# Key-query products of two heads issued alternately on 32-column tiles, decayed operands in two products, and one rounded gate product

## The chip, the cores and the metric

The kernel runs on one core of a Trainium2 chip. The engines of that core are TensorE (PE in the profile; PEld is its loading of weights), VectorE (DVE), ScalarE (ACT), GpSimd (POOL) and SyncE (SP), which issues DMAs. They run side by side and meet through semaphores. The metric is the device time of one execution in microseconds; the figure for a kernel is the median of its runs.

## The reference, cut to what matters

One layer of a streaming encoder is computed for 1024 prompt tokens and 32 sample tokens. The change lies in its gated linear attention: four heads, key width 64, value width 128, with a decay for each token and key channel.

```python
glog = jax.nn.log_sigmoid((glr @ w_gate2 + b_gate2)) / GLA_GATE_TEMP      # glr: 16 columns of h @ w_in
b = jnp.cumsum(g, axis=2)
o_inter = jnp.einsum('bhid,bhde->bhie', q * jnp.exp(b), S)
diff = b[:, :, :, None, :] - b[:, :, None, :, :]
decay = jnp.exp(jnp.where(causal[None, None, :, :, None], diff, -jnp.inf))
att = jnp.einsum('bhid,bhjd,bhijd->bhij', q, k, decay)
o = o_inter + jnp.einsum('bhij,bhje->bhie', att, v)
S_new = jnp.exp(b_last[:, :, 0, :])[..., None] * S + jnp.einsum('bhjd,bhje->bhde', k * jnp.exp(b_last - b), v)
```

Around it stand the input projection (queries, keys, values, an output gate, a second group of mixers), the output projection and an MLP of width 4096 with two LayerNorms.

## The kernel before

The kernel has three stages. The first (up to about 115 us in the profile) normalizes the input and forms part of the projections. The second, in which the change lies, forms the rest of the projections, runs the attention and begins the output projection; it ends near 407 us. The third does the remaining output projection and the MLP, up to 1218 us. Big products keep each operand as a rounded high part and a rest (type fp32r) and take three passes; small ones are plain fp32, and the profile records two matmuls (and two weight loads) for each plain fp32 product, one for an fp32r product.

Tokens are cut into three blocks of 384, 384 and 288, and a block into windows: eight windows of 128 prompt tokens and one of 32 sample tokens. The four heads are two pairs (pair 0, pair 1), so there are 18 rounds of window and pair. Windows are numbered 0 to 8 here; in pair 0 they run first. Two heads of a pair lie on partitions 0 to 63 and 64 to 127.

- `gate` makes, for a block and pair, the running sum of log decays (`b`) and differences inside groups of four (`dd`): a product of 16 by 128 weights with 384 columns (L703), three ACT functions, and a row of DVE work.
- `elem` makes the decayed queries and keys of a window. For each of five levels (blocks of 64, 32, 16, 8, 4 tokens) POOL subtracts running sums (L748, L749), one ACT exponential covers all levels (L755, shown under the helper's line L608; 128x640), and DVE multiplies the later half of each block by the queries (L761) and the earlier half by the keys (L762). `x` holds four more products. `z` and `x` share the buffer `zx`, of which there are two, so `elem` of window n+2 starts when window n is done with its buffer.
- `gram` makes the attention matrix: for each head, 16 products of 32x32 at levels 16, 8, 4 and inside the groups of four (L783), one of 64x64 (L786) and two of 32x32 (L790), all on 64 rows of the PE array. The PE then transposes the decayed keys (L793). DVE picks the causal parts out of PSUM under masks into `cmp` (L797), copies the four diagonal blocks into `att` (L805), ACT copies one off-diagonal block (L800) and DVE two (L802).
- `outp` makes the state increment (L817), the part of the output from the state (L821) and from `att` (L824), and updates the state on DVE (L830). `gla_norm` normalizes (ACT, POOL), the PE transposes (L851), and DVE multiplies into `mix` (L854).
- `mix_split` splits `mix` into high and rest (ACT L943, DVE and POOL L944) for the output projection.
- `ada_stream` (114 to 203 us) streams 24 weight tiles through the buffers `wad` and `zx` and reduces them on DVE.

The order on the PE is written out by a planner (`Order`): each part of the work is a stream with a priority, and a `yield (a, b)` says that it took the PE a nanoseconds and wants to go on b nanoseconds later; in between, streams of lower priority (projections) put their matmuls. These matmuls are called fill here. The order on DVE, ACT and POOL comes from the framework's scheduler, which uses its own estimate of times. Each engine runs its instructions strictly in its order.

## Time and profile before

| | |
|---|---|
| median of 3 runs | 1217.69 us (1216.70 to 1219.08) |
| the profiled execution's own time | 1219.88 us |
| its span in the profile | 1218.1 us |
| mean granted PE clock | 0.98 |
| PE busy | 1169.3 us, 96% of the span |
| DVE busy | 909.8 us, 75% |
| first and last key-query product | 240.7 and 384.8 us |

The page gives busy time by engine, the span in 40 slices, the DMA queues, a chain of waits and the costliest groups of instructions. A busy PE is one with some matmul in flight; matmuls overlap, so the length of a piece of PE work is read from one start to the next. In rows of instructions in order of time the columns are start and length in us, engine, line, operation, output<-inputs, array rows*columns, shapes, count, and in brackets the idle time before and what ended it.

### The profile page before, as it was taken

The numbers are of one execution on the slowest core, as the hardware profiler recorded it, in microseconds if no ns is written. First come the engines' busy times: TensorE is split into PE (matmuls) and PEld (weight loads), VectorE is DVE, ScalarE is ACT, GpSimd is POOL, SyncE is SP. The second block draws the span as 40 slices with busy tenths as digits, with TensorE's granted clock in tenths as the row PEclk, the third lists the DMA queues.
The fourth block names the chain that finished last, engine by engine and source line by source line (L and its number), as shares of the span: only waits on it lengthen the run. The fifth ranks groups of instructions, "written<-read, shape, count | busy, mean of one in ns | idle before, by whom it ended". The sixth has DMA issues, their size and how long they took to land.

```text
span 1218.1 us, 22199 instructions
## 1 busy us (share of the span) xinstructions
PE 1169.3 (96%) x8539; PEld 1114.4 (91%) x8539; DVE 909.8 (75%) x1905; ACT 521.2 (43%) x1065; POOL 469.4 (39%) x682
## 2 busy tenths in 40 slices
PE   5999999999899999899989999999999999999996
PEld 3678999988788999799989999999999999999996
DVE  5664797579896688756759769589499597697577
ACT  4462322446566665642425343343443443433321
POOL 2443110345684154348541442334414414422034
PEclk9999999999899999889989999999999999999998
DMA  9632564110012765204762672743825726737412
GB/s 370 239 126 90 180 214 125 36 36 20 23 37 76 263 219 165 83 31 169 251 242 70 210 252 91 244 171 120 300 100 184 265 70 207 246 100 226 157 73 104
DMA packets 49498, 188.46 MB, mean 155 GB/s; under 512 B 5328, under 2 KB 10928, under 8 KB 49392
## 3 DMA queue, kind: packets, MB, share of 16 engines
q1 hardware_dynamic: 31824, 97.38, 23.4%
q0 software_dynamic: 17568, 89.66, 21.5%
q8 instruction: 67, 1.10, 0.4%
q14 instruction: 39, 0.32, 0.1%
HBM read 171.36 MB, written 15.66 MB: 154 GB/s over the span
## 4 chain that ended last, share of the span: by engine, by line
PE 76%; DVE 11%; DMA 4%; POOL 3%; ACT 2%; issue 2%; SPq 0%; POOLq 0%; DVEq 0%; ACTq 0%
PE mm L250 26%; PE mm L1375 16%; PE mm L1442 12%; PE mm L1236 9%; PE mm L284 3%; PE zp L284 3%; DVE hl L1039 2%; DMA raw<-in_w_dram 2%; DVE acc L1467 1%; DMA wst<-in_w_dram 1%; PE zp L250 1%; DMA tdT<-hl 1%; PE mm L1142 1%; PE gt L783 1%; PE mm L227 1%
## 5 line engine op out<-in xcount | busy, mean ns | idle before, releaser
L1038 ACT CAST hl<-raw 128x512 fp32r<-128x512 f32 (+1 forms) x238 | 143.7, 613 | 242.9 <-PE mm L1442 93.3
L1039 DVE TENSOR_TENSOR hl<-raw,hl 128x512 fp32r<-128x512 f32 (+1 forms) x238 | 203.5, 861 | 40.8 <-ACT hl L1038 40.8
L1375 PE MATMUL mm<-ring,hl 128*128 128x384 f32 x960 | 173.7, 338 | 3.4 <-DMA ring<-tdT 3.4
L1375 PEld LDWEIGHTS mm<-ring,hl 128*128 128x128 f32 x960 | 168.9, 190 | 3.8 <-issue 3.7
L1442 PE MATMUL mm<-ring,hl 128*128 128x384 f32 x792 | 140.8, 335 | 1.3 <-DVE acc L1467 1.3
L1442 PEld LDWEIGHTS mm<-ring,hl 128*128 128x128 f32 x792 | 137.5, 188 | 1.9 <-ACT ring L1038 1.4
L250 PE MATMUL mm<-hT,whl 128*128 128x384 f32 (+1 forms) x792 | 129.0, 322 | 0.0
L250 PEld LDWEIGHTS mm<-hT,whl 128*128 128x128 f32 x792 | 127.0, 188 | 1.1 <-issue 1.1
L250 PE MATMUL mm<-h,hl 128*128 128x288 f32 (+1 forms) x756 | 122.3, 318 | 1.7 <-POOL h L239 1.4
L250 PEld LDWEIGHTS mm<-h,hl 128*128 128x128 f32 x756 | 115.4, 196 | 4.6 <-POOL h L239 3.6
L1083 POOL TENSOR_TENSOR raw<-raw 128x512 f32<-128x512 f32 x26 | 35.9, 1383 | 184.7 <-DMA raw<-in_w_dram 155.3
L1467 DVE SCALAR_TENSOR_TENSOR acc<-mm,G,acc 128x384 f32<-128x384 f32 x162 | 93.7, 607 | 5.4 <-PE mm L1442 4.8
L1236 PE MATMUL mm<-fb,hl 128*128 128x288 f32 x708 | 97.0, 295 | 0.0
L1236 PEld LDWEIGHTS mm<-fb,hl 128*128 128x128 f32 x708 | 95.4, 188 | 0.0
L1247 DVE SCALAR_TENSOR_TENSOR acc<-mm,G,acc 128x256 f32<-128x256 f32 (+3 forms) x176 | 61.8, 390 | 12.0 <-PE mm L1236 11.8
L250 PE MATMUL mm<-mhl,hl 128*128 128x384 f32 (+1 forms) x384 | 65.3, 325 | 2.0 <-ACT hl L1038 1.8
L250 PEld LDWEIGHTS mm<-mhl,hl 128*128 128x128 f32 x384 | 60.3, 192 | 2.6 <-ACT hl L1038 2.1
L1323 POOL DMA_DIRECT2D ring<-tdT x56 | 31.3, 560 | 71.8 <-PE mm L1375 38.2
L284 PE MATMUL zp<-zvw,hT 128*128 128x512 f32 x192 | 52.9, 418 | 4.5 <-ACT hT L236 4.5
L1399 DVE TENSOR_TENSOR tmps<-mm,tmps 128x384 f32<-128x384 f32 x28 | 15.6, 558 | 50.4 <-PE mm L1375 50.4
L1345 ACT CAST ring<-F 128x768 fp32r<-128x768 f32 x42 | 35.1, 837 | 40.0 <-DVE F L1337 20.0
L217 POOL TENSOR_SCALAR rs<-mv 128x1 f32<-128x1 f32 (+1 forms) x27 | 8.6, 322 | 111.1 <-DVE mv L216 108.5
(253 smaller groups left out, 2282.2 us busy)
## 6 DMA issues: line engine op xcount, KB each, us to landing
ring<-tdT POOLq DMA_DIRECT2D x56, 768.0 KB, 5.9
raw<-in_w_dram SPq DMA_DIRECT2D x80, 512.0 KB, 3.9
ring<-tdB POOLq DMA_DIRECT2D x42, 768.0 KB, 6.4
wst<-in_w_dram SPq DMA_DIRECT2D x34, 512.0 KB, 4.4
wad<-in_w_dram POOLq DMA_DIRECT2D x24, 512.0 KB, 4.6
tdT<-hl SPq DMA_DIRECT2D x16, 384.0 KB, 2.9
st<-in_w_dram SPq DMA_DIRECT2D x10, 512.0 KB, 10.2
tdB<-h SPq DMA_DIRECT2D x6, 768.0 KB, 4.4
```

The lines of the kernel that those rows point to most:

```text
L250: PE.matmul(pt[:, :n], h[:, a, 128 * kk:128 * kk + 128], act[:, b_, k, :n], start=(i == 0 and j == 0), stop=(i == 7 and j == 2))
L284: PE.matmul(pt[:n, :width], act[:, a, k, off:off + n], hl[:, b_, width * kk:width * kk + width], start=(k == 0 and a + b_ == 0), stop=(k = ...
L1038: S.copy(hl[:, 0, :n], src)
L1039: V.tensor_tensor(hl[:, 1, :n], src, hl[:, 0, :n].bitcast(F32), ALU.subtract)
L1083: G.tensor_tensor(s, a21, a22, ALU.add)
L1236: PE.matmul(pt[:, :n], hl[kk // 2][:, a, o_:o_ + 128], f(kk)[:, c_], start=(kk == 0 and j == 0), stop=(kk == 3 and j == 2))
L1247: V.scalar_tensor_tensor(ac, pt[:, o + lo - p0:o + hi - p0], G2[:, m, c:c + 1], ac, ALU.mult, ALU.add)
L1323: G.dma_start(s, td[t, j].rearrange("p (a c) -> p a c", a=2))))
L1345: S.copy(q[:, 0], src)
L1375: PE.matmul(pt[:, :384], hl[:, a, o_:o_ + 128], quad(ts[j])[:, b_, kk], start=first and j + kk + i == 0, stop=j + kk + i == 4, skip_group_ ...
L1442: PE.matmul(pt[:, :384], hl[:, a, o_:o_ + 128], f[:, b_, kk], start=first and kk + i == 0, stop=kk + i == 3, skip_group_check=True)
L1467: V.scalar_tensor_tensor(ac, v, G2[:, m, 0:1], ac, ALU.mult, ALU.add)
```

## The change

Four things change, all in the second stage.

1. In `gram` the products of the two heads alternate, product by product, and all of them use tiles of 32 columns: the 64x64 product becomes two of 32x64. The diagonal blocks are put into `att` by one product of `cmp` with a block-diagonal matrix of ones (`bd`), which writes all of `att`; the copies of the off-diagonal blocks follow it.
2. In `elem` the ten half-block multiplications become two over all levels: queries times `z` into a new buffer `zq` (there is one), keys times `z` in place. Both halves are now computed, and the products read the half they need.
3. In `gate` the low-rank activations are kept as a rounded high part (twice) and a rest, stacked on 96 partitions against high, high and rest of the weights, so that one fp32r product of 96 rows takes the place of one plain fp32 product of 16 rows. For pair 0 this adds an ACT copy and a DVE subtraction per block.
4. The planner is told that a key-query round takes 950 (700 for the window of 32) in place of 1700, and that `outp` comes 3800 in place of 3200 later. To make room, `b` has 3 buffers in place of 4 and `wad` 1 in place of 2, with more of the weight tiles going through `zx`.

```diff
-            wg2 = pb.tile([96, 256], F32, name="wg2")
+            wg2 = pb.tile([P, 2, 128], F32, tag="on", name="wg2", bufs=2)[:96].rearrange("p a b -> p (a b)")
...
-            glr = pb.tile([96, 384], F32, name="glr")
+            bd = pb.tile([P, 1, 4, 32], F32, name="bd")
+            glr = [pb.tile([96, BLK[b][1]], F32R, name=f"glr{b}") for b in range(3)]
+            wsp = pb.tile([96, 256], F32R, name="wsp")
...
+                S.copy(wsp, wg2)
+                V.tensor_tensor(wsp[64:96], wg2[64:96], wsp[64:96].bitcast(F32), ALU.subtract)
...
-                        V.tensor_copy(glr[r, :n], pt[:16, :n])
-                        yield 330, 1000
+                        gl = glr[b]
+                        V.tensor_copy(gl[0:16], pt[:16, :n])
+                        S.copy(gl[64:80], pt[:16, :n])
+                        V.tensor_tensor(gl[32:48], pt[:16, :n], gl[0:16].bitcast(F32), ALU.subtract)
+                        yield 330, 1500
                     pt = mm()
-                    PE.matmul(pt[:, :n], wg2[r, 128 * p:128 * p + 128], glr[r, :n], start=True, stop=True,
-                              tile_position=(32 * b, 0))
+                    PE.matmul(pt[:, :n], wsp[:, 128 * p:128 * p + 128], glr[b], start=True, stop=True)
...
-                    bb = pb.tile([P, 384], F32, tag="b", name="b", bufs=4)
+                    bb = pb.tile([P, 384], F32, tag="b", name="b", bufs=3)
...
-                for i in range(l0, 5):
-                    s = LV[i]
-                    zz = zs[i - l0]
-                    V.tensor_tensor(zz[:, :, 1], zz[:, :, 1], hv(q, s)[:, :, 1], ALU.mult)
-                    V.tensor_tensor(zz[:, :, 0], zz[:, :, 0], hv(k, s)[:, :, 0], ALU.mult)
+
+                zq = pb.tile([P, 5, 128], F32, tag="zq", name="zq", bufs=1)
+                lv = lambda t: t.rearrange("p (o t) -> p o t", o=1).to_broadcast([P, 5 - l0, w])
+                V.tensor_tensor(zq[:, l0:5, :w], z[:, l0:5, :w], lv(q), ALU.mult)
+                V.tensor_tensor(z[:, l0:5, :w], z[:, l0:5, :w], lv(k), ALU.mult)
...
-                for hd in range(2):
-                    r = slice(64 * hd, 64 * hd + 64)
-                    for li in range(4):
-                        kz, qz = (z[:, li + 2], z[:, li + 2]) if li < 3 else (x[:, 1], x[:, 0])
-                        for g in range(w // 32):
-                            cs = slice(32 * g, 32 * g + 32)
-                            PE.matmul(gt[32 * g:32 * g + 32, hd, 32 * li:32 * li + 32], kz[r, cs], qz[r, cs],
-                                      start=True, stop=True, tile_position=(64 * hd, 32 * g))
-                    if w == 128:
-                        PE.matmul(gt[0:64, hd, 128:192], z[r, 0, 0:64], z[r, 0, 64:128],
-                                  start=True, stop=True, tile_position=(64 * hd, 0))
...
+                def grams(kz, qz, parts):
+
+                    for o_, cs, d_ in parts:
+                        for hd in range(2):
+                            r = slice(64 * hd, 64 * hd + 64)
+                            PE.matmul(gt[o_:o_ + 32, hd, d_:d_ + cs.stop - cs.start], kz[r, o_:o_ + 32], qz[r, cs],
+                                      start=True, stop=True, tile_position=(64 * hd, o_))
+                for li in range(4):
+                    grams(*((z[:, li + 2], zq[:, li + 2]) if li < 3 else (x[:, 1], x[:, 0])),
+                          [(o_, slice(o_, o_ + 32), 32 * li) for o_ in range(0, w, 32)])
+                if w == 128:
+                    grams(z[:, 0], zq[:, 0], [(o_, slice(64, 128), 128) for o_ in (0, 32)])
+                    grams(z[:, 1], zq[:, 1], [(o_, slice(o_ + 32, o_ + 64), 192) for o_ in (64, 0)])
...
+                    V.tensor_tensor(att.rearrange("p h (c t) -> p h c t", c=4), cmp.rearrange("p h (c t) -> p h c t", c=1)
+                                    .to_broadcast([P, 2, 4, 32]), bd.to_broadcast([P, 2, 4, 32]), ALU.mult)
...
-                for g in range(w // 32):
-                    V.tensor_copy(att[32 * g:32 * g + 32, :, 32 * g:32 * g + 32], cmp[32 * g:32 * g + 32])
+                else:
+                    V.tensor_copy(att[:32, :, :32], cmp[:32])
...
-                        yield (1700 if w == 128 else 1700), 200
+                        yield (950 if w == 128 else 700), 200
...
-                        yield 0, 3200
+                        yield 0, 3800
...
-                    if i % 4 < 2:
-                        w = pb.tile([P, D], F32, tag="wad", name="wad", bufs=2)
+                    if i % 3 == 0:
+                        w = pb.tile([P, D], F32, tag="wad", name="wad", bufs=1)
```

The order of instructions moves in three places. The first is one round of key-query products on the PE (a window of 128); `gt` is the PSUM tile they write, and L793 (now L800) is the transpose behind them. Before:

```order
L783 MATMUL gt<-zx 32x32 x16
L786 MATMUL gt<-zx 64x64
L790 MATMUL gt<-zx 32x32 x2
L783 MATMUL gt<-zx 32x32 x16
L786 MATMUL gt<-zx 64x64
L790 MATMUL gt<-zx 32x32 x2
L793 MATMUL mm<-ident,zx 128x128
```

Now:

```order
L791 MATMUL gt<-zq,zx 32x32 x24
L791 MATMUL gt<-zx 32x32 x8
L791 MATMUL gt<-zq,zx 32x64 x4
L791 MATMUL gt<-zq,zx 32x32 x4
L800 MATMUL mm<-ident,zx 128x128
```

The 38 products have become 40, and no product uses 64 columns of the array.

The second is the PE around the `outp` of window 4 of pair 1, where `hs` and `mhl` are operands of fill (values of the last window, and the output projection). Before, 16 matmuls with `hs` (their last row stands here) and 12 with `mhl` lie between the key-query round and `outp`:

```order
L276 MATMUL mm<-whl,hs 64x256
L250 MATMUL mm<-mhl_3832,whl 128x384 x12
L817 MATMUL mm<-v,ks 64x128 x2
L821 MATMUL o<-st_1223,zx 128x256
L824 MATMUL o<-v,att_1211 128x128 x2
L783 MATMUL gt<-zx 32x32 x16
L786 MATMUL gt<-zx 64x64
L790 MATMUL gt<-zx 32x32 x2
L783 MATMUL gt<-zx 32x32 x16
L786 MATMUL gt<-zx 64x64
L790 MATMUL gt<-zx 32x32 x2
L793 MATMUL mm<-ident,zx 128x128
```

Now (the first three rows are `outp` of window 3, then the round of window 4 and its `outp`):

```order
L826 MATMUL mm<-v,ks 64x128 x2
L830 MATMUL o<-st_1227,zx 128x256
L833 MATMUL o<-v,att_1214 128x128 x2
L791 MATMUL gt<-zq,zx 32x32 x24
L791 MATMUL gt<-zx 32x32 x8
L791 MATMUL gt<-zq,zx 32x64 x4
L791 MATMUL gt<-zq,zx 32x32 x4
L800 MATMUL mm<-ident,zx 128x128
L860 MATMUL o<-ident,on 128x128 x2
L826 MATMUL mm<-v,ks 64x128 x2
L830 MATMUL o<-st_1227,zx 128x256
L833 MATMUL o<-v,att_1215 128x128 x2
```

Window 4 has no fill now; window 3 has 12 matmuls of it, and the windows before took more than they did.

The third is DVE at the same window 4 of pair 1. Before, from the products of window 5 to the copies of two off-diagonal blocks of window 4 (L802):

```order
L761 TENSOR_TENSOR zx<-zx,q 128x64
L762 TENSOR_TENSOR zx<-zx,k 128x64
L761 TENSOR_TENSOR zx<-zx,q 128x2x32
L762 TENSOR_TENSOR zx<-zx,k 128x2x32
L761 TENSOR_TENSOR zx<-zx,q 128x4x16
L762 TENSOR_TENSOR zx<-zx,k 128x4x16
L761 TENSOR_TENSOR zx<-zx,q 128x8x8
L762 TENSOR_TENSOR zx<-zx,k 128x8x8
L761 TENSOR_TENSOR zx<-zx,q 128x16x4
L762 TENSOR_TENSOR zx<-zx,k 128x16x4
L141 TENSOR_TENSOR whl<-wst,whl 128x512 x2
L802 COPY att_1211<-gt 32x2x32 x2
```

Now, from the masked picks of window 4 to the same copies (L811), with `zq` (L769) and the key product (L770) of window 5, the first products of window 6 (L764, L765) and the state update of window 4 (L839) ahead of them:

```order
L804 COPY_PREDICATED cmp_1217<-msk,gt 128x64 x2
L769 TENSOR_TENSOR zq<-zx,q 128x640
L807 TENSOR_TENSOR att_1215<-cmp_1217,bd 128x256
L839 SCALAR_TENSOR_TENSOR st_1227<-st_1227,el,mm 64x128 x2
L953 TENSOR_TENSOR mhl_3669<-mix_859,mhl_3669 128x384
L770 TENSOR_TENSOR zx<-zx,k 128x640
L764 TENSOR_TENSOR zx<-zx,q 128x128
L765 TENSOR_TENSOR zx<-zx,k 128x128
L811 COPY att_1215<-gt 32x2x32 x2
```

Ten products have become two, and the copies that `outp` waits for stand behind more work of later windows than before.

More of the change, by code (lines that the diff above doesn't have):

```diff
@@ L599, in consts_b @@
                 G.memset(cb_[:, 0:1], 1.0)
-                for t in att_t + cmp_t:
+                for t in att_t + cmp_t + [g_.bitcast(F32) for g_ in glr] + [bd]:
                     G.memset(t, 0.0)
+                for g in range(4):
+                    G.memset(bd[32 * g:32 * g + 32, :, g], 1.0)
+                S.copy(wsp, wg2)
+                V.tensor_tensor(wsp[64:96], wg2[64:96], wsp[64:96].bitcast(F32), ALU.subtract)
             exp_set, gtok = [], []
@@ L692, in gate @@
                     yield lambda: prs[0].elem + prs[1].elem >= 3 * (3 * p + b - 1)
-                    r = slice(32 * b, 32 * b + 16)
                     if not p:
@@ L765, in elem @@
                 pr.elem += 1
-                return z, x, el
+                return (z, zq), x, el
             wcount, behind = [0], {}
@@ L771, in gram @@
                 off, w, c = WIN[b][wi]
-                z, x, el = zx
+                (z, zq), x, el = zx
                 gw = wcount[0]
@@ L776, in gram @@
                 gt = psb.tile([P, 2, 512], F32, tag="g", name="gt", bufs=1)
-                for hd in range(2):
-                    r = slice(64 * hd, 64 * hd + 64)
-                    for li in range(4):
-                        kz, qz = (z[:, li + 2], z[:, li + 2]) if li < 3 else (x[:, 1], x[:, 0])
-                        for g in range(w // 32):
-                            cs = slice(32 * g, 32 * g + 32)
-                            PE.matmul(gt[32 * g:32 * g + 32, hd, 32 * li:32 * li + 32], kz[r, cs], qz[r, cs],
-                                      start=True, stop=True, tile_position=(64 * hd, 32 * g))
-                    if w == 128:
-                        PE.matmul(gt[0:64, hd, 128:192], z[r, 0, 0:64], z[r, 0, 64:128],
-                                  start=True, stop=True, tile_position=(64 * hd, 0))
-                        for g in range(2):
-                            o2 = 64 * g
-                            PE.matmul(gt[o2:o2 + 32, hd, 192:224], z[r, 1, o2:o2 + 32], z[r, 1, o2 + 32:o2 + 64],
-                                      start=True, stop=True, tile_position=(64 * hd, o2))
+                def grams(kz, qz, parts):
[10 more added lines that the diff above has]
+                    grams(z[:, 1], zq[:, 1], [(o_, slice(o_ + 32, o_ + 64), 192) for o_ in (64, 0)])
                 kt = mm()
```

## The prediction

> **What bounds the kernel now.** I read the busy times first, then how the stage with the change looks on the PE in order of time, then who waited for whom there, and last DVE's work in stretches of that stage.
>
> ```profile
> PE 1169.3 (96%) x8539; PEld 1114.4 (91%) x8539; DVE 909.8 (75%) x1905; ACT 521.2 (43%) x1065; POOL 469.4 (39%) x682
> PE gt L783 <- DVE zx L762: 4.3, 5, 3.3
> PE o L824 <- DVE att L802: 1.2, 1, 1.2
> 274.70:289.70 15.00, 15.00 (x223) 12.68 (x222) 13.83 (x58) 8.80 (x35) 10.04 (x31) 1.00 0.01 3
> 289.70:305.10 15.40, 15.21 (x236) 12.86 (x236) 14.12 (x58) 10.14 (x39) 7.51 (x27) 1.00 0.11 36
> ```
>
> The PE is the bound. The two rows of waits are all that it lost to another engine from 235 to 395 us: 5.5 us (total, times, longest). The last two rows are stretches of the stage: span, then busy time of PE, PEld, DVE, ACT, POOL, the granted clock, DMA. DVE is busy 13.83 of 15.00 us: a close second, which caps what a shorter PE can bring there.
>
> **The key-query round.** This is one window of 128 on the PE, each row one run of matmuls of a line:
>
> ```profile
> 240.71 0.46 PE L783 MATMUL gt<-zx 64*32 64x32 f32 x32
> 241.10 0.32 PE L786 MATMUL gt<-zx 64*64 64x64 f32 x2
> 241.35 0.22 PE L790 MATMUL gt<-zx 64*32 64x32 f32 x2
> 241.81 0.33 PE L786 MATMUL gt<-zx 64*64 64x64 f32 x2
> 242.06 0.25 PE L790 MATMUL gt<-zx 64*32 64x32 f32 x4
> 242.24 0.33 PE L793 MATMUL mm<-ident,zx 128*128 128x128 f32 x1
> L783 PE MATMUL gt<-zx x1056: 190/193/256, 240.7 to 384.8; 64*32 64x32 f32 x176
> 305.06 0.59 PE L783 MATMUL gt<-zx 64*32 64x32 f32 x16
> 305.58 0.28 PE L793 MATMUL mm<-ident,zx 128*32 128x128 f32 x1
> ```
>
> From its start to the transpose the round takes 242.24-240.71 = 1.53 us. The 32 records of one head last 0.46 us, one alone 0.193 (the middle of its three durations), so they start 0.27/32 = 8.4 ns apart. Each 64x64 product holds the array for 241.35-241.10 = 0.25 us, though it has two records only: that is the cost of going to 64 columns and back. In the small window (the last two rows) each head has one column tile, and 16 records take 0.52 us, 32 ns each: a column tile is slower to reuse than the stream of four is to issue.
>
> After the change there are 80 records, all on 32 columns. At 8.4 ns they take 0.67 us; the way into the transpose costs 242.24-242.06 = 0.18 us less four records, 0.15. That makes 0.82, so 0.71 saved, times 16 = 11.4 us. Bounds: if the two heads run fully side by side, 4.2 ns per record give 0.49 and a saving of 1.04, 16.6 in all; if only the 64 records of L783 keep their 0.54 and the other 16 cost what L786 and L790 cost now (0.75 over both heads), 0.24 saved, 3.8 in all. I take 11.4: it uses the measured pace and only drops the changes of tile size. In the two small windows two row tiles can halve the 0.52: 0.25 each, 0.5 in all (at worst 0).
>
> The Trainium skill ("TensorE: Matmul & The Clock Gate", "Wait — 56ns, not 53.3ns?") says that starts of matmuls are never under about 25 ns apart. By that, 80 records would need 2.0 us, more than now, and the 16 rounds would lose some 7 us. The trace disagrees: 76 records went in 1.53 us, 20 ns each with the stops included.
>
> **The gate product.** Six times in the stage; the first two rows are one of them and what follows it, the third is a run of rounded products of 384 columns:
>
> ```profile
> 213.75 0.91 PE L703 MATMUL mm<-glr,wg 16*128 16x384 f32 x2
> 214.58 7.82 PE L284 MATMUL mm<-whl,hT 128*128 128x272 f32 x60
> 378.63 4.43 PE L250 MATMUL mm<-mhl,whl 128*128 128x384 f32 x24
> ```
>
> It takes 0.83 us; a rounded product of this width takes 4.43/24 = 0.18. So 0.65 saved in the four wide blocks; in the two of 288 columns three quarters of it, 0.49. That is 3.6 us (2.4 if 0.4 is all that each saves). The extra copy and subtraction of the first block lie beside the 60 records of the second row, those of the others beside later fill; uncovered, each would cost some 0.5 us.
>
> PE work saved: 11.4 + 0.5 + 3.6 = 15.5 us.
>
> **The old stalls.** The 5.5 us above had an after-effect, a slower array:
>
> ```profile
> 323.30 0.33 PE L783 MATMUL gt<-zx 64*32 64x32 f32 x16 [3.31 <-DVE zx L762]
> 326.65 6.40 PE L284 MATMUL mm<-whl,hT 128*128 128x256 f32 x36
> 336.26 4.53 PE L284 MATMUL mm<-whl,hT 128*128 128x256 f32 x36
> 359.32 0.68 PE L824 MATMUL o<-v,att 128*128 128x128 f32 x4 [1.23 <-DVE att L802]
> 361.95 5.83 PE L250 MATMUL mm<-mhl,whl 128*128 128x384 f32 x24
> 319.10:334.40 15.30, 11.65 (x128) 9.62 (x127) 12.54 (x40) 5.66 (x20) 5.26 (x9) 0.78 0.00 1
> ```
>
> After a wait of 3.31 us the same 36 matmuls took 6.40 in place of 4.53, with a granted clock of 0.78 in that stretch; after 1.23 us, 24 took 5.83 in place of 4.43. That is 1.87 + 1.40 = 3.3 us. If the new order removed all of this, 5.5 + 3.3 = 8.8 us would come back too.
>
> **What is late next.** The order puts 12 matmuls of fill into window 3 of pair 1 and none into window 4, and on DVE the copies that `outp` of window 4 needs stand behind products of window 5. How long that chain is, from the state product on (L821, which frees the buffer for the window after next):
>
> ```profile
> 368.08 0.70 PE L821 MATMUL o<-st,zx 128*128 128x256 f32 x2
> 368.86 0.40 POOL L741 TENSOR_TENSOR zx<-b 128x128 f32<-128x128 f32 x1 [4.00 <-PE o L821]
> 371.95 0.74 ACT L608 ACTIVATE zx<-zx 128x640 f32<-128x640 f32 x1 [0.63 <-POOL zx L749]
> 382.99 0.44 PE L817 MATMUL mm<-v,ks 128*64 128x128 f32 x4
> 383.36 0.70 PE L821 MATMUL o<-st,zx 128*128 128x256 f32 x2
> 383.90 0.61 PE L824 MATMUL o<-v,att 128*128 128x128 f32 x4
> 384.43 0.59 PE L783 MATMUL gt<-zx 64*32 64x32 f32 x16
> ```
>
> The exponentials of the next buffer are there 371.95+0.74-368.08 = 4.6 us after L821 began. DVE's pieces:
>
> ```profile
> 356.32 0.21 DVE L762 TENSOR_TENSOR zx<-zx,k 128x64 f32<-128x64 f32 x1
> 357.40 0.21 DVE L762 TENSOR_TENSOR zx<-zx,k 128x64 f32<-128x64 f32 x1
> 296.05 1.29 DVE L141 TENSOR_TENSOR whl<-wst,whl 128x512 fp32r<-128x512 f32 x2
> 352.11 0.40 DVE L757 TENSOR_TENSOR zx<-zx,k 128x128 f32<-128x128 f32 x1
> 354.06 0.79 DVE L805 COPY att<-cmp 32x64 f32<-32x64 f32 x4
> 351.13 0.71 DVE L830 SCALAR_TENSOR_TENSOR st<-st,el,mm 64x128 f32<-64x128 f32 x2
> 348.92 0.44 DVE L802 COPY att<-gt 32x64 f32<-32x64 f32 x2
> ```
>
> The ten old products start (357.40-356.32)/8 = 0.135 us apart: 1.35 a window. A product of 512 elements takes 1.29/2, so one of 640 about 0.8 at most, 0.75 taken: two make 1.5. That is 0.15 more, not less, since each now covers both halves. The four diagonal copies (0.79) become one product of 256 elements, about 0.4 (twice 128 elements of L757 less its overhead). DVE saves 0.25 us a window, 4 us in the stage.
>
> Window 4, counted from L821 of window 3: exponentials at 4.6, `zq` 0.75, the `att` product 0.4, state update 0.71, a `mhl` subtraction 0.6, the key product 0.75, two first products of window 6 0.65, the copies 0.44: 8.9 us. The PE meanwhile has L821 and L824 (384.43-383.36 = 1.07), a round (0.82), two transposes (0.5), L817 (0.37) and L821 (0.54): 3.3 us. It waits 5.6. Window 3, the same way: 4.6 + 0.75 + 0.44 = 5.8 against 3.3 plus 12 fill at 0.18, 5.5: 0.3. Together 5.9 us, and the slow clock behind it: more than the 1.87 of a 3.31 wait, I take 3.0. The other windows have 24 or more of fill (4.4 us), so the PE gets there after 7.7 us and the chain of 5.8 to 6.5 is covered.
>
> Two smaller costs. In 274.7 to 305.1 the PE would need 15.00 and 15.40 less two rounds and a gate product (2.07), 12.93 and 13.33; DVE needs 13.83 and 14.12 less 0.5, 13.33 and 13.62: 0.7 us lost together. And POOL's `mhl` subtractions, beside which a DVE product stood still, come again:
>
> ```profile
> 319.59 3.52 DVE L761 TENSOR_TENSOR zx<-zx,q 128x64 f32<-128x64 f32 x1
> 320.14 2.88 POOL L944 TENSOR_TENSOR mhl<-mix,mhl 128x384 fp32r<-128x384 f32 x3
> ```
>
> Their place is now beside window 1 of pair 1, which has 48 fill: between 0 and the old 3.3; I take 1.3.
>
> Past the stage the PE's order is the same as before, so I carry the difference to the end. The weight stream through fewer buffers ends before the attention, 37 us ahead of the first round: 0.
>
> ```profile
> L899 DVE DVE_READ_ACCUMULATOR wad<-wad,csb x24: 80/83/88, 133.9 to 203.3; 128x1 f32 x24
> ```
>
> **Sum.** -15.5 - 8.8 + 5.9 + 3.0 + 0.7 + 1.3 = -13.4 us. From the profiled execution's 1219.88: 1206.5. The median of the runs lies 2.2 lower, so 1204 us is predicted.
>
> **Rivals.**
> - *The wait at window 4 stays small* (its copies come early enough, or the PE arrives later): 8.9 us are not paid, 1195. For it: the PE reached `outp` with only one wait of 1.23 in the whole stage. Against: the order itself. 0.15.
> - *POOL pays for the long DVE products*: each of two products of 0.75 us holds off POOL's subtractions, as L944 held off L761, and the exponentials come up to 1.5 us later. The chain of 6.5 becomes 8.0 against 7.7, and with the gate's DVE work in every third window more; some 0.5 us in 14 windows, 7 us: 1211. The Trainium skill ("SBUF — State Buffer", "SBUF: two separate sides") speaks for it: a DVE operation with two SBUF inputs and a reading GpSimd operation exclude each other for a whole instruction. The row of 3.52 us agrees. 0.20.
> - *The round does not get shorter* beyond its lower bound, 3.8: 1212. Against: the 0.25 us stops at L786 are plain. 0.08.
> - *Slower*: `att` copies wait for the next window's exponentials in every window, and the chain exceeds the fill. It decides from 7.7 us on; at 9.2 us 14 windows lose 1.5 each, 21 us with no clock counted: 1204 + 21 = 1225. Against: 4.6 us to the exponentials is measured with POOL loaded. 0.04.
> - *No difference*: the round goes by the count of its records, 1.53/76 = 20 ns each, whatever the tiles; 80 take 1.61, and 11.4 + 1.3 us are missing from the forecast: 1217. Against: the 8.4 ns inside a run. A floor under the starts, as in the page named above, is of this kind. 0.03.
>
> The forecast has 0.50. Its own range is 1199 to 1209; with the neighbours the range is 1195 to 1213. About 0.2% (2.4 us) is what a measurement of this kernel can tell from no change. Faster by more: 0.50+0.15+0.20+0.08 = 0.93, given as 0.92; same 0.04; slower 0.04.
>
> **What would show it.** Right: a round of 0.7 to 0.9 us from its first product to the transpose; gate products near 0.2; one long PE wait for `att` at window 4 of pair 1, none over 1 us in pair 0; the last key-query product near 378 us in place of 384.8 (13.4 earlier, with 36 more matmuls of fill, 6.5 us, ahead of it). Wrong: a round over 1.1 us, waits for `att` or `zx` in most windows, or POOL subtractions much over 0.3 us beside L769 and L770.

## The result

The changed kernel takes 1209.72 us (median of 4 runs, 1208.49 to 1211.02), the kernel before 1218.38 us beside it (4 runs, 1216.70 to 1220.77). The ratio is 0.9929, with a 95% interval of 0.9913 to 0.9944: faster by 0.7%, 8.7 us. The forecast was 1204, 13.4 us less, with a range of 1195 to 1213. Sign and range hold; a third of the gain is missing. The profiled execution took 1210.69 us, its span is 1208.8 (before 1219.88 and 1218.1): 9.2 to 9.3 us less.

Lines have moved: the key-query products, all on L791 now, were L783, L786 and L790. L712 (gate product) was L703, L800 (key transpose) L793, L811 (`att` copies) L802, L833 (product with `att`) L824, L830 (state product) L821, L860 (output transposes) L851, L953 (`mhl` subtraction) L944, L615 (exponentials) L608, L857 (scaled output) L848, L1047 (cast of the next stage's weights) L1038. L769 and L770 are the two long products.

### The profile page after: what moved, and what is told of

It is laid out like the page before. It is cut to its first block, busy times and chain, and to the rows that moved or that the text cites. A ratio compares the mean times of both kernels' runs of the same rounds, so it can differ in the third digit from the quotient of the medians.

```text
span 1208.8 us, 22157 instructions
## 1 busy us (share of the span) xinstructions
PE 1152.5 (95%) x8597; PEld 1103.3 (91%) x8597; DVE 907.3 (75%) x1725; ACT 522.6 (43%) x1069; POOL 483.9 (40%) x690
## 4 chain that ended last, share of the span: by engine, by line
PE 77%; DVE 11%; DMA 3%; POOL 3%; issue 3%; ACT 2%; SPq 0%; DVEq 0%; POOLq 0%; ACTq 0%
PE mm L250 26%; PE mm L1384 16%; PE mm L1245 11%; PE mm L1451 11%; PE zp L284 3%; DVE hl L1048 3%; PE mm L284 3%; DVE acc L1476 2%; DMA raw<-in_w_dram 1%; PE zp L250 1%; DMA tdT<-hl 1%; PE mm L1151 1%; DMA wst<-in_w_dram 1%; PE mm L227 1%; DVE acc L1256 1%
## 5 line engine op out<-in xcount | busy, mean ns | idle before, releaser
L1047 ACT CAST hl<-raw 128x512 fp32r<-128x512 f32 (+1 forms) x238 | 144.5, 613 | 247.7 <-PE mm L1451 95.4
L1256 DVE SCALAR_TENSOR_TENSOR acc<-mm,G,acc 128x256 f32<-128x256 f32 (+3 forms) x176 | 61.5, 387 | 11.9 <-PE mm L1245 11.8
```

The source lines that it names most:

```text
L1047: S.copy(hl[:, 0, :n], src)
L1256: V.scalar_tensor_tensor(ac, pt[:, o + lo - p0:o + hi - p0], G2[:, m, c:c + 1], ac, ALU.mult, ALU.add)
```

## The profile after

Busy times come from the first part of the page. The PE is 17 us less busy, DVE 2.5 us, POOL 14.5 us more.

```profile
PE 1152.5 (95%) x8597; PEld 1103.3 (91%) x8597; DVE 907.3 (75%) x1725; ACT 522.6 (43%) x1069; POOL 483.9 (40%) x690
```

The timeline of the PE (start, duration) shows a gate product, the first round and a small one (a window of 32), each with what follows it:

```profile
215.17 0.34 PE L712 MATMUL mm<-glr,wsp 96*128 96x384 f32 x1
215.35 0.29 PE L284 MATMUL mm<-whl,hT 128*128 128x272 f32 x1
...
239.06 0.59 PE L791 MATMUL gt<-zq,zx 64*32 64x32 f32 x45
...
239.89 0.33 PE L800 MATMUL mm<-ident,zx 128*128 128x128 f32 x1
...
302.18 0.38 PE L791 MATMUL gt<-zq,zx 64*32 64x32 f32 x12
...
302.55 0.29 PE L800 MATMUL mm<-ident,zx 128*32 128x128 f32 x1
```

The gate product takes 215.35-215.17 = 0.18 us, a round 239.89-239.06 = 0.83, a small one 0.37 (0.52 before).

The waits of the PE from 235 to 395 us (total, times, longest) were two rows with 5.5 us before. Now they are these five and two more of 0.4 and 0.3, 12.0 us:

```profile
PE o L833 <- DVE att L811: 6.4, 3, 5.1
PE o L860 <- ACT on L857: 2.3, 1, 2.3
PE gt L791 <- DVE zx L770: 1.1, 3, 0.7
PE o L833 <- ACT zx L615: 0.9, 1, 0.9
PE mm L712 <- DVE glr L709: 0.6, 1, 0.6
```

Where the three longest lie, and what follows them, again from the PE's timeline:

```profile
322.88 0.42 PE L860 MATMUL o<-ident,on 32*128 32x32 f32 x2 [2.27 <-ACT on L857]
323.63 5.59 PE L284 MATMUL mm<-whl,hT 128*128 128x256 f32 x36
...
345.51 0.68 PE L833 MATMUL o<-v,att 128*128 128x128 f32 x4 [0.93 <-DVE att L811]
...
354.45 1.19 PE L833 MATMUL o<-v,att 128*128 128x128 f32 x4 [5.11 <-DVE att L811]
355.57 0.71 PE L791 MATMUL gt<-zq,zx 64*32 64x32 f32 x44
...
356.77 2.27 PE L250 MATMUL mm<-mhl,whl 128*128 128x384 f32 x6
358.83 0.63 PE L860 MATMUL o<-ident,on 128*128 128x128 f32 x2
359.11 4.99 PE L250 MATMUL mm<-mhl,whl 128*128 128x384 f32 x24
```

354.45 is window 4 of pair 1, 345.51 is window 3. DVE's timeline ahead of 354.45 is the chain that the forecast wrote down; the pieces left out are the product for `att`, the state update, a `mhl` subtraction and the two first products of window 6:

```profile
349.92 0.82 DVE L769 TENSOR_TENSOR zq<-zx,q 128x640 f32<-128x640 f32 x1 [0.94 <-ACT zx L615]
...
352.33 0.91 DVE L770 TENSOR_TENSOR zx<-zx,k 128x640 f32<-128x640 f32 x1
...
353.85 0.45 DVE L811 COPY att<-gt 32x64 f32<-32x64 f32 x2
```

The PE's timeline at the end of the stage, first before, then after:

```profile
401.12 5.50 PE L250 MATMUL mm<-mhl,whl 128*128 128x384 f32 x30
408.41 0.62 PE L250 MATMUL mm<-mhl,hl 128*128 128x384 f32 x2 [1.79 <-ACT hl L1038]
409.22 3.14 PE L250 MATMUL mm<-mhl,hl 128*128 128x384 f32 x9 [0.20 <-DVE hl L1039]
```

```profile
390.34 6.50 PE L250 MATMUL mm<-mhl,whl 128*128 128x384 f32 x36
396.77 0.31 PE L860 MATMUL o<-ident,on 32*128 32x32 f32 x2
401.26 0.98 PE L250 MATMUL mm<-mhl,hl 128*128 128x384 f32 x2 [4.19 <-ACT hl L1047]
404.38 4.79 PE L250 MATMUL mm<-mhl,hl 128*128 128x384 f32 x16 [2.14 <-DVE hl L1048]
```

The stage ends at 401.12+5.50 = 406.62 before and 396.77+0.31 = 397.08 now, 9.5 us earlier. But the next stage then waits 4.19 + 2.14 us where it waited 1.79 + 0.20: 4.3 us of the 9.5 are gone at once. As much comes back later: from 410 to 500 us the PE waited 7.6 us before and waits 4.9 now, and near 620 us 2.3 in place of 3.4. The rows of the view of waits, before, then after:

```profile
PE mm L1142 <- ACT y L952: 6.6, 2, 5.6
PE mm L227 <- ACT xr L1183: 1.0, 1, 1.0
PE mm L1375 <- DMA ring<-tdT: 3.4, 1, 3.4
```

```profile
PE mm L227 <- ACT xr L1192: 3.7, 1, 3.7
PE mm L1151 <- ACT y L961: 1.2, 1, 1.2
PE mm L1384 <- DMA ring<-tdT: 2.3, 1, 2.3
```

-9.5 + 4.3 - 2.7 - 1.1 = -9.0, against the 9.2 to 9.3 seen. These are the largest rows, not a full account: the wait for `h` from POOL (L239), for one, grows from 1.4 to 2.2 us.

## Experiments

Theory at the start: the PE time is gone as forecast, and the rest was lost in two places, at windows 3 and 4 (12 and 0 matmuls of fill) and at the stage's end. Rivals: POOL pays for the long DVE products and sets the pace; or the next stage is bound elsewhere and takes back what comes early. Then the parts of the change were run one by one. Each was timed beside the kernel before, in 4 runs; turns alone has 7 and the gate product alone 10.

"Waits" below is the sum of the PE's waits from the first gate product to the last matmul of the stage; "end" is when the stage's last matmul ends; "tail" is how many matmuls of fill stand behind the last product with `att` (L833), and "start" the waits of the next stage's first weights. These four are read from one profiled execution each.

| kernel | round us | waits us | end us | tail | start us | median us | ratio to before, 95% |
|---|---|---|---|---|---|---|---|
| before | 1.53 | 5.5 | 406.6 | 84 | 2.0 | 1218.4 | 1 |
| the change | 0.83 | 12.0 | 397.1 | 48 | 6.3 | 1209.7 | 0.9929 (0.9913, 0.9944) |
| late buffer | 0.83 | 11.8 | 397.3 | 48 | 6.5 | 1210.6 | 0.9934 (0.9917, 0.9952) |
| even fill | 0.83 | 8.8 | 393.0 | 84 | 2.0 | 1203.2 | 0.9871 (0.9851, 0.9892) |
| even fill, late buffer | 0.83 | 10.7 | 395.3 | 84 | 1.9 | 1204.9 | 0.9884 (0.9861, 0.9906) |
| old numbers | 0.83 | 15.0 | 401.2 | 84 | 2.0 | 1209.7 | 0.9924 (0.9907, 0.9942) |
| 32 columns alone | 0.94 | 7.4 | 402.4 | 84 | 2.0 | 1208.8 | 0.9922 (0.9898, 0.9945) |
| turns alone | 1.15 | 4.5 | 396.2 | 84 | 2.0 | 1212.4 | 0.9955 (0.9939, 0.9972) |
| round alone | 0.83 | 6.9 | 395.3 | 84 | 2.0 | 1204.9 | 0.9889 (0.9858, 0.9921) |
| gate product alone | 1.53 | 8.9 | 407.4 | 84 | 2.0 | 1219.9 | 1.0003 (0.9990, 1.0016) |
| ten products | 0.83 | 10.4 | 396.8 | 48 | 6.7 | 1210.4 | 0.9936 (0.9916, 0.9955) |
| even more | 0.83 | 8.2 | 392.3 | 30 | 6.3 | 1208.0 | 0.9914 (0.9881, 0.9947) |
| even fill, DVE | 0.83 | 9.2 | 393.3 | 84 | 2.0 | 1201.0 | 0.9858 (0.9820, 0.9895) |
| the same, small products | 0.83 | 10.3 | 395.6 | 84 | 2.0 | 1206.3 | 0.9894 (0.9869, 0.9918) |

Behind the stage the program is the same in all of them but for addresses of buffers, yet from the next stage's first matmul on it took 809.7 us in the kernel before and 803.9 to 808.5 in the others. Why is open. So part of what the totals gain lies behind the stage, and "end" and "start" together say more about an edit inside it.

### Late buffer

In the changed kernel a weight load of the next stage waits on SP's queue for L860, because `on` now lies where that load goes:

```profile
SPq L1104 <- PE o L860: 4.8, 1, 4.8
```

```diff
-            wg2 = pb.tile([P, 2, 128], F32, tag="on", name="wg2", bufs=2)[:96].rearrange("p a b -> p (a b)")
+            wg2 = pb.tile([P, 256], F32, tag="v", name="wg2", bufs=9)[:96]
```

> The changed kernel with one edit: the gate weights are staged in a buffer of the values v in place of one of the normalised outputs on, so that on moves to another address. Theory (the boundary): in the changed kernel the second weight load of the third stage waits for the last transposes that read on, and the PE then waits 4.19 and 2.14 us for the first pieces. With on elsewhere these two waits fall under 1 us together, the third stage begins 4 to 5 us earlier and the time falls from 1209.7 to about 1206. Rival (the third stage is bound by DVE and ACT until about 485 us, whatever the PE does at its start): the two waits fall as well, but the wait for y near 484 us grows from 1.23 to 4 to 5 us, and the time stays within 1 us of 1209.7.

The three loads now go out one after the other, without that wait, but the PE waits as it did (SP's timeline with the last store of the state, then the PE's):

```profile
388.07 1.10 SPq L842 DMA_DIRECT2D out_dram<-st  x2
...
391.88 2.85 SPq L1104 DMA_DIRECT2D raw<-in_w_dram  x3
```

```profile
401.49 0.77 PE L250 MATMUL mm<-mhl,hl 128*128 128x384 f32 x2 [4.24 <-ACT hl L1047]
```

Neither theory holds: the address does not cause the waits at the start, so this run says nothing on what they cost. The time is that of the change. The loads go out sooner and land no sooner: from 395 to 405 us the DMA engines are busy throughout in both kernels (a share of 1.01 in the change and 1.02 here, by the profile), and among the transfers of 386 to 405 us the loads of these weights took 8.5 us from issue to landing here (median) and 6.8 there. What goes with the waits shows in the next runs.

### Even fill, and old numbers

```diff
-                        yield (950 if w == 128 else 700), 200
+                        yield (950 if w == 128 else 700), 0
```

> The changed kernel with one number: the next window's operands are due 0 ns after a round in place of 200, which spreads the fill as 30 30 24 24 24 24 30 36 36, 36 36 36 36 28 24 24 24 24 over the 18 windows, so that no window is left with 12 or 0. Theory (the fill): the wait of 5.1 us at window 4 of pair 1 and the 0.9 us at window 3 go, with the slow clock behind them; all PE waits from the first round to the stage's end fall from 12.0 to about 5 us, the stage ends 6 to 9 us earlier, and the time is about 1203 if the next stage carries it. Rival (POOL and DVE hold each other off, and the chain of a window is longer than its fill everywhere): the waits scatter over the windows of 24, their sum stays at 9 us or more, and the time at 1207 to 1210.

1203.2 us, 6.5 under the change, as the first theory said. No wait is over 1.8 us; the largest row for L833 is:

```profile
PE o L833 <- DVE att L811: 3.1, 3, 1.1
```

But 8.8 us of waits are more than the 5 expected, spread over many windows, as the rival said. The stage ends 4.1 us earlier than in the change, where the theory had 6 to 9. And the tail is back at 84, with 2.0 us at the start of the next stage, 4.3 us less than in the change. That gain stands in no term of the theory, so its time is in part luck.

With the late buffer too:

> Both edits: even fill, and the gate weights staged in a buffer of v. If fill and boundary are separate costs that both carry to the end, this is the sum of the two single runs: about 1199 to 1201. If the third stage's start is bound by DVE and ACT, it stands within 1 us of the even fill alone.

It gains nothing further (1204.9; the intervals overlap). The buffer's address is out.

The old numbers give each window the fill that it had before:

```diff
-                        yield (950 if w == 128 else 700), 200
+                        yield (1700 if w == 128 else 1700), 200
...
-                        yield 0, 3800
+                        yield 0, 3200
```

(and 1000 for the gate's 1500.)

> The changed kernel with the planner's numbers of before (1700 for both windows, 3200, 1000): every window then has the fill that it had before, 30 36 30 30 18 24 30 24 36, 36 36 36 36 28 24 24 24 24. Theory (the fill): the waits at windows 3 and 4 of pair 1 go as with the even fill; the window of 18 may wait about 0.5 us; waits of 4 to 6 us in all and about 1203 to 1205. Rival (the new numbers gain by themselves, or POOL sets the pace): waits of 9 us or more and 1208 to 1212.

1209.7 us: the rival's number, and no window lacks fill. The waits are 15.0 us, none over 3.1; the row with the longest:

```profile
PE o L860 <- ACT on L857: 3.8, 2, 3.1
```

So the new numbers are not what loses the gain: without them the stage ends 4.1 us later than in the change, and many waits of about 1 us stand where one of 5.1 and the start of the next stage stood. With a round shorter by 0.7 us the PE comes to many windows before the other engines are through.

### The round in parts

32 columns alone is the kernel before with this edit:

```diff
-                        PE.matmul(gt[0:64, hd, 128:192], z[r, 0, 0:64], z[r, 0, 64:128],
-                                  start=True, stop=True, tile_position=(64 * hd, 0))
+                        for o2 in (0, 32):
+                            PE.matmul(gt[o2:o2 + 32, hd, 128:192], z[r, 0, o2:o2 + 32], z[r, 0, 64:128],
+                                      start=True, stop=True, tile_position=(64 * hd, o2))
```

> The kernel before with one edit: its 64x64 key-query product of each head is written as two products on 32-column tiles; heads one after the other, ten DVE products, old gate product, old numbers. Theory (the stops are the change of tile size): 80 records and no change of size leave 1.53 less two stops of 0.25 us, about 1.05 us for a round. PE work falls by 16 times 0.48, 7.7 us; since the run with the old numbers showed that about half of such a saving comes back as waits, the time is 1212 to 1215 from 1217.9. Rival (the stops come from the heads, or the round goes by its records): the round stays at 1.4 us or more and the time within 1 us of before.

Turns alone keeps the 64x64 product and lets the heads take turns:

```diff
-                for hd in range(2):
-                    r = slice(64 * hd, 64 * hd + 64)
-                    for li in range(4):
+                for li in range(4):
...
+                        for hd, r in enumerate(hr):
                             PE.matmul(gt[32 * g:32 * g + 32, hd, 32 * li:32 * li + 32], kz[r, cs], qz[r, cs],
...
```

> The kernel before with one edit: the two heads take turns product by product, and the 64x64 products stay on 64-column tiles. Theory (stops by tile size): the two 64x64 products stand side by side, one change of size each way in place of two, so the round takes about 1.53 less 0.25 to 0.35 us, 1.2. If the two heads run fully side by side as well (4.2 ns a record), about 0.9 to 1.0. Time 1213 to 1216. Rival (alternation gains nothing, all of the changed round comes from the tile size): 1.5 us and the time of before.

Their rounds, from the PE's timeline (32 columns, then turns):

```profile
241.00 0.46 PE L783 MATMUL gt<-zx 64*32 64x32 f32 x32
...
241.94 0.33 PE L794 MATMUL mm<-ident,zx 128*128 128x128 f32 x1
```

```profile
240.26 0.76 PE L783 MATMUL gt<-zx 64*32 64x32 f32 x64
240.95 0.33 PE L787 MATMUL gt<-zx 64*64 64x64 f32 x4
241.21 0.27 PE L792 MATMUL gt<-zx 64*32 64x32 f32 x8
241.41 0.33 PE L795 MATMUL mm<-ident,zx 128*128 128x128 f32 x1
```

One product written as two takes the round from 1.53 to 0.94, with four records more. Turns alone give 1.15, and the stop at the 64x64 products stays at 0.26, once in place of twice. Both together save 0.70, not the sum of 0.97: part of what turns save is a stop, and that is gone already. In total, 32 columns alone is as fast as the whole change, and its 1208.8 is below the expected 1212 to 1215. But 16 times 0.59, 9.4 us of PE work, ended the stage only 4.2 us earlier than before, against 9.5 in the change: waits grew by 1.9 us, and the granted clock from 300 to 340 us was 0.87 in place of 0.91. Of the 10.0 us that its span is shorter, 5.8 lie behind the next stage's first matmul, in the part that is open. That the ratio gives 9.5 us, so near the 9.4, is chance as far as these runs tell. Turns alone took from 1207.1 to 1214.4 us in 7 runs, in two groups; the profile is of the lower one, so its few waits may not stand for the rest.

The round alone has both edits, and all else as before.

> The kernel before with the round of the change alone: heads take turns and all products stand on 32-column tiles; ten DVE products, four diagonal copies, old gate product, old numbers. Theory (the round carries the whole gain, and the rest of the change gives nothing): the round takes 0.83 us, and the time is 1208 to 1211, as the changed kernel. Rival (the long products, the product for att and the gate product give part of it): 1212 or more. If the fill theory alone held, with this fill of 24 to 36 per window, it would be under 1206; the run with the old numbers (1209.7) speaks against that.

1204.9 us, under the numbers of theory and rival, where the fill theory alone had put it. Its runs lie from 1203.7 to 1206.1, those of the change from 1208.5 to 1211.0, though the two intervals of the ratio overlap a little (0.9913 to 0.9921). The kernel with the old numbers has the same fill and differs by the long products, the product for `att`, the gate product and the buffers; it waits 15.0 us where this one waits 6.9, ends the stage 6.0 us later, and takes 4.8 us more. So beside these numbers those edits take back 4.8 us of what the round gives.

### Gate product alone

```diff
-            glr = pb.tile([96, 384], F32, name="glr")
+            glr = [pb.tile([96, BLK[b][1]], F32R, name=f"glr{b}") for b in range(3)]
+            wsp = pb.tile([96, 256], F32R, name="wsp")
...
-                    PE.matmul(pt[:, :n], wg2[r, 128 * p:128 * p + 128], glr[r, :n], start=True, stop=True,
-                              tile_position=(32 * b, 0))
+                    PE.matmul(pt[:, :n], wsp[:, 128 * p:128 * p + 128], glr[b], start=True, stop=True)
```

(and the split of both operands, and the weight tiles through one `wad` buffer, as in the change.)

> The kernel before with the gate product over stacked rounded parts, and the weight stream of the modulation through one buffer less, which makes room for it; all else as before. Theory (PE time counts): the six gate products take 0.2 to 0.3 us in place of 0.83, 3.6 us of PE work are gone, and 1214 to 1216 us result. Rival (a window's chain of DVE, ACT and POOL sets the pace, so PE time taken away there comes back as waits): the products are as short, PE waits grow by 2 us or more, and the time stays within 1.5 us of before.

No gain: 1.0003 (0.9990 to 1.0016). The product is short, but the PE now waits for its split, and once more for a copy into `att` (its timeline, then the new rows of waits):

```profile
258.03 0.40 PE L709 MATMUL mm<-glr,wsp 96*128 96x288 f32 x1 [1.77 <-DVE glr L706]
```

```profile
PE mm L709 <- DVE glr L706: 2.4, 3, 1.8
PE o L829 <- DVE att L810: 0.9, 1, 0.9
```

The waits grow by 3.4 us in all, against the 3.6 us of work that were expected to go, and the stage ends 0.8 us later than before. That is the rival's reading.

### Ten products

```diff
-                V.tensor_tensor(zq[:, l0:5, :w], z[:, l0:5, :w], lv(q), ALU.mult)
-                V.tensor_tensor(z[:, l0:5, :w], z[:, l0:5, :w], lv(k), ALU.mult)
+                zq = z
+                for i in range(l0, 5):
...
+                    V.tensor_tensor(zz[:, :, 1], zz[:, :, 1], hv(q, s)[:, :, 1], ALU.mult)
+                    V.tensor_tensor(zz[:, :, 0], zz[:, :, 0], hv(k, s)[:, :, 0], ALU.mult)
```

> The changed kernel with the ten small DVE products in place of the two long ones (in place, without zq); numbers and fill as changed. Theory (two long products are no dearer): POOL's key product and powers go back by 0.1 to 0.2 us each, DVE has 0.2 to 0.4 us more a window, the wait at window 4 stays at 5 us or grows, and the time is 1209 to 1213. Rival (POOL pays for the long products, and the chain with it): POOL's busy time in the stage falls by 8 us or more, the waits of the PE fall from 12.0 to 9 us or less, and the time to 1204 to 1207.

POOL does pay for the long products: one of its groups in the stage, the powers of the norm, with them (the change), then without:

```profile
L855 POOL TENSOR_TENSOR ms<-ms,mhalf 128x2 f32<-128x2 f32 x16 | 15.4, 960 | 0.6
```

```profile
L857 POOL TENSOR_TENSOR ms<-ms,mhalf 128x2 f32<-128x2 f32 x16 | 11.9, 746 | 0.6
```

From 239 to 392 us POOL is busy 100.9 with and 89.9 without, more than the 8 us that the rival asked for. The waits, though, are 10.4 and the time 1210.4: what POOL pays did not set the time here. The theory's number holds.

### Even more, and the fill behind the last window

```diff
-                        yield 0, 3800
+                        yield 0, 4000
```

(on the even fill.)

> The changed kernel with the next window's operands due at 0 ns, as in the even fill, and outp due 4000 ns after them in place of 3800: fill 30 36 30 30 24 30 42 36 36, 36 36 36 34 24 30 30 30 30, and none behind the last transposes. Theory (a window's chain of some 7.5 to 8 us needs 27 to 30 matmuls of fill beside a round of 0.83, and the fill behind the last transposes covers the way to the next stage): the waits inside the stage fall from 10.6 us with the even fill to 4 to 7, but the third stage begins with waits of 4 to 6 us in place of 2.0, so the time is within 2 us of the even fill, 1201 to 1205. Rival (the waits depend on where POOL's subtractions fall, not on the fill): the waits inside the stage stay at 9 to 12 us and the time is 1205 to 1208.

The 10.6 in that text counts the 1.79 at the next stage's start; inside the stage the even fill has 8.8. Here it is 8.2, hardly less with 30 to 36 matmuls in nearly every window. But one of the waits is of the fill itself, for a `mhl` subtraction on POOL:

```profile
PE mm L250 <- POOL mhl L953: 2.8, 1, 2.8
```

Without it 5.4 us are left, within the theory's 4 to 7. So more fill did shorten the windows' waits, and a subtraction of POOL made a new one, which is the rival's point; so is the time, 1208.0. The start of the next stage differs too:

```profile
398.60 1.66 PE L250 MATMUL mm<-mhl,hl 128*128 128x384 f32 x3 [6.34 <-ACT hl L1047]
```

The time is 4.8 us above the even fill. Across all fourteen kernels this splits cleanly: ten have a tail of 84 and wait 1.9 to 2.0 us there; four have 48 or 30 and wait 6.3 to 6.7. That 30 costs no more than 48 shows that the wait is not simply the missing fill. In the change ACT's cast of those weights waits for their load, here in its timeline:

```profile
400.07 1.14 ACT L1047 CAST hl<-raw 128x512 fp32r<-128x512 f32 x2 [1.81 <-DMA raw<-in_w_dram]
```

The loads stand in SP's queue behind the store of the last window's state (387.91 in the change, 388.07 with the late buffer above), so they go out after the last window, and on the PE it is the tail that covers them. That the loads of the late buffer land no earlier goes with the full DMA engines; no run took other transfers away to test it.

### DVE in place of POOL, and small products again

In the change, L770 takes 3.83 us in one place, where it took 0.91 at 352.33 above, beside three of POOL's subtractions (DVE's timeline, then POOL's):

```profile
322.73 3.83 DVE L770 TENSOR_TENSOR zx<-zx,k 128x640 f32<-128x640 f32 x1
```

```profile
322.96 2.91 POOL L953 TENSOR_TENSOR mhl<-mix,mhl 128x384 fp32r<-128x384 f32 x3
```

```diff
-                        (G if k % 2 else V).tensor_tensor(t[:, 1, k], mix[b][:, k], t[:, 0, k].bitcast(F32), ALU.subtract)
+                        (G if k % 2 and b else V).tensor_tensor(t[:, 1, k], mix[b][:, k], t[:, 0, k].bitcast(F32), ALU.subtract)
```

(on the even fill: the first block's subtractions all on DVE.)

> The changed kernel with the even fill, and the three mhl subtractions of the first token block that POOL makes are made by DVE too. In the even fill one DVE product (L770) takes 3.84 us beside these three in place of 0.82. Theory (the two engines exclude each other, and that stretch costs the PE): no DVE operation over 2 us in the stage; DVE does 2 us more and is freed of 3; the waits near 316 to 323 us (1.77 and 0.88) shrink and the time is 1 to 3 us under the even fill, 1200 to 1202. Rival (the chain there is set by DVE's work, not by its standing still): the same waits or more, 1203 to 1206.

No such stretch is left, L770 takes 857 ns in the mean in place of 1073 in the even fill, and the time is 1201.0, the best of all and the theory's number. But its reason is not borne out: the waits are 9.2, not fewer, and the one for L857 that was to shrink grew from 1.8 to 2.7 us. The interval overlaps that of the even fill, so that it beats the even fill is not shown. Beside the change (0.9929) its interval, 0.9820 to 0.9895, lies wholly below.

On top of it the small DVE operations of before, the ten products as above and four diagonal copies:

```diff
-                    V.tensor_tensor(att.rearrange("p h (c t) -> p h c t", c=4), cmp.rearrange("p h (c t) -> p h c t", c=1)
-                                    .to_broadcast([P, 2, 4, 32]), bd.to_broadcast([P, 2, 4, 32]), ALU.mult)
...
+                for g in range(w // 32):
+                    V.tensor_copy(att[32 * g:32 * g + 32, :, 32 * g:32 * g + 32], cmp[32 * g:32 * g + 32])
```

> The kernel of the last run (even fill, the first block's subtractions on DVE) with the DVE work of before put back: the ten small products in place and four diagonal copies of att, in place of two long products and one product. The round of 0.83 us, the gate product and the fill stay. Theory (the long DVE products cost the PE: the copies for att stand behind a product of 0.82 to 1.1 us, and POOL is held off by it; the round alone gave 1204.9 at nearly this fill, and all the edits together 1209.7): the waits for L811's copies fall from 3.5 us to about 2, those of the stage from 9.2 to 5 to 7, and the time to 1197 to 1200. Rival (the gate product's split makes the difference between those two runs, not DVE's products): the waits stay at 8 us or more and the time at 1200 to 1203.

1206.3: outside both expectations, 5.2 us slower, with no run of the one within the runs of the other. Only 2.4 us of it show at the stage's end, and 3.4 of the 5.8 by which the spans differ lie behind the next stage's first matmul. So here the new DVE work as a whole (the long products and the one for `att`) helps a little, if anything beyond chance; at the change's numbers the long products made no difference, and beside the round alone they were among the edits that cost 5 us. Their price seems to depend on the order around them, and these runs do not settle by what.

## Why the prediction was right, and where not

*The round*: 0.82 forecast, 0.83 measured. The reason given, that the stops at the change of tile size go, carries most of it, 0.59 of 0.70. But by that reason the 80 records would take 0.82 head after head, and they take 0.94: the pace is 9.9 ns then, and the turns, from which the forecast took nothing, make up the 0.11. The Trainium skill ("TensorE: Matmul & The Clock Gate", "Wait — 56ns, not 53.3ns?") has starts never under about 25 ns; here 80 went in 0.83 us, 10 ns each, and the measurement decides. The Trainium skill ("TensorEngine Tiling (Array Packing)", "Key Properties") also says that a change of tiling mode drains the array; the run with 32 columns alone agrees, with 0.59 us less for a round.

*PE work*: 15.5 forecast. The stage ends 9.5 us earlier with 6.5 us more waits, and the slow clock behind waits is 0.5 less (2.8, below): 9.5 + 6.5 - 0.5 = 15.5. The term held, though 15.5 is what is left over in this sum; the rounds alone, read directly, give 16 times 0.70 and twice 0.15, 11.5 of the 11.9 forecast.

*The gate product* was priced right (0.18 where fill follows at once) and its split wrong: "beside later fill" cost 0.65 us in the change and 2.4 in the run of its own, and alone the edit gave nothing.

*Window 4*: 5.6 forecast, 5.11 measured; window 3 0.3 and 0.93. DVE's part is the chain that was written down, 4.38 us from the exponentials to the copies for 4.3. But the start of it was not, as the state product of window 3 and the exponentials show (the PE's timeline, then ACT's):

```profile
343.88 0.70 PE L830 MATMUL o<-st,zx 128*128 128x256 f32 x2
```

```profile
349.15 0.74 ACT L615 ACTIVATE zx<-zx 128x640 f32<-128x640 f32 x1 [1.34 <-POOL zx L757]
```

The exponentials came 349.15+0.74-343.88 = 6.0 us after L830, not 4.6, and the PE was ready for the product 5.5 us after it, not 3.3. The 4.6 came from one window; in the two windows ahead of that one the same step had taken 6.0 and 6.4. The two errors nearly cancel, so the near hit is partly luck.

*The slow clock* behind new waits: 3.0 forecast. The granted clock was 0.89 from 320 to 335 us and 0.78 from 355 to 367. 36 matmuls took 5.59 in place of 4.53, 6 took 2.06 in place of 1.08, 24 took 4.99 in place of 4.43, a round 1.07: 2.8.

*The other new waits* are the mis-sized term. Forecast 0.7 for DVE's load and 1.3 for POOL's subtractions, 2.0 with 5.9 for the windows, 7.9 in all; measured 12.0. The largest piece, 2.27 us at 322.88 for L857, was in no term, nor was the 0.65 of the gate. L857 stood behind POOL's powers (L855, 321.44 to 322.12 us), and these behind ten of POOL's subtractions. The difference is 4 us, and it takes the stage from -13.4 to the -9.5 seen.

*"Past the stage the PE's order is the same as before, so I carry the difference to the end"* failed as a step, though it cost little in the end. The order is the same, but what lies ahead of it is not: the 36 matmuls that were moved ahead of the last round no longer stand behind it, and the next stage's first weights, covered before, were waited for, 4.3 us. That the next stage then waited 2.7 + 1.1 us less elsewhere is chance of this case as far as these runs tell; from its first matmul on, the rest of the program took 804 to 810 us in the fourteen profiles.

*The signs.* The round, the wide gate products, and the one long wait for `att` came as listed, and no wait in pair 0 was over 0.65 us. The last key-query product started at 381.8 us, not near 378, which is the 4 us of waits again. Of the signs of being wrong one came in part: single subtractions of POOL beside L770 took far over 0.3 us (0.90 at 317.15), though the mean rose only from 0.32 to 0.34.

*The rivals.* The two on the round, a small saving or none, are out by its 0.83 us, and *slower* by the result. The wait at window 4 can be had small, as the first rival said, by one number, but the time is then 1203.2, not 1195. That POOL pays for the long products is true as a mechanism: 11 us of its time in the stage, and at window 4, where ten small products bring the exponentials after 4.8 us in place of 6.0. It did not set the time here: with the ten products the wait at window 4 is 5.12 us and the time 1210.4, against 5.11 and 1209.7. The Trainium skill ("SBUF — State Buffer", "SBUF: two separate sides") says that a DVE operation with two SBUF inputs and a GpSimd operation that reads SBUF exclude each other for a whole instruction; the rows of 3.83 us on DVE and 2.91 us on POOL agree.

## What to carry to other kernels

Keep small products on one tile size: leaving the 64-column tile took 0.59 of the 0.70 us off a round. Judge an edit by the end of the stage it lies in, too: here totals gained up to 5.8 us behind it in a part that no edit touched. When the bound engine gets faster inside a pipeline its waits grow, here from 5.5 to between 7 and 15 us in all runs but one, and which edit helps depends on the others; so run them one by one as well as together. Work that is moved ahead of a stage's last step is missing behind it, where it may have covered the next stage's first load. And a step of a chain that was measured in one window should be measured in the others before a forecast rests on it.

## What the runs showed of the hardware that was not expected

The two heads on two row tiles add little once all products have one column width: 0.83 against 0.94 us. In the small window, where each head has one column tile, turns take 16 records from 0.52 to 0.37 us.
